# The softmax reciprocals of the forgetting attention, moved from VectorE to POOL as a power of minus one

## The chip, the cores and the metric

The kernel runs on one core of a Trainium2 chip. A core has five engines that run side by side, each with a queue of its own that is worked off in order: TensorE (PE in the profile, its weight loads PEld), VectorE (DVE), ScalarE (ACT), GpSimd (POOL) and SyncE (SP, which only issues transfers here). The metric is the device time of one execution in microseconds. Before the change the median of 3 runs was 1450.64 us (1450.14 to 1451.19).

## The reference

One encoder layer on x of 1024 tokens by 1024 channels, in float32: a mixer (forgetting attention beside gated linear attention), cross-attention to 256 memory tokens, and a squared-ReLU MLP, each behind an RMS norm and added to the residual. The change is in the forgetting attention (8 heads of 64 channels):

```python
for i in range(S // Q_BLOCK):                       # Q_BLOCK = 128
    start, end = i * Q_BLOCK, (i + 1) * Q_BLOCK
    s = jnp.einsum('bqhd,bkhd->bhqk', q[:, start:end], k[:, :end]) * scale
    bias = c[:, :, start:end, None] - c[:, :, None, :end]
    s = jnp.where(mask, s + bias, -jnp.inf)
    p = jax.nn.softmax(s, axis=-1)
    outs.append(jnp.einsum('bhqk,bkhd->bqhd', p, v[:, :end]))
```

A block of 128 queries sees only the keys up to its own end, so the eight blocks of a head are 128, 256, ... 1024 keys wide. The reciprocal in question is that of the softmax: one per query, 128 in a block, 64 blocks in all.

## The kernel before

All matrix products are float32 products made of three passes of split operands (`gemm`, L110 to L112). The stages follow each other: projections of the mixer (to about 315 us), forgetting attention (315 to 559 us), output projection, cross-attention (from about 600 us), and the MLP, which is more than half of the time.

The forgetting attention works by head, and in a head by blocks in the order 0, 4, 1, 5 (`fox_group` of group 0), then 2, 6, 3, 7. For each block `fox_scores` (L645 to L668) does this:

- TensorE writes the scores into PSUM (L656, L657, and the mask, L659). There is one PSUM tile for blocks of up to 512 keys (`s1`) and one for the wider ones (`s2`), so the next block of a kind waits until the exponential of the last one has read it.
- VectorE takes the negative row maximum (L661).
- ACT writes the exponential into `p` and sums it into `rs` (L664).
- VectorE takes the reciprocal of `rs`, 128x1 (L666).
- POOL multiplies `p` by it in place (L667).

Then `values` (L683) transposes `p` on TensorE (L696), ACT and VectorE split the transposes into a rounded part and a rest (`evac_split`, L117 and L118, three PSUM tiles `tr`), TensorE multiplies them with the values (L703, L704), and ACT and VectorE add the two halves (L706, L709).

Between these steps TensorE works on side work (`side_work`, L733): two parts of the output projection and the keys and values of the cross-attention. It is recorded in small pieces between the blocks, and its weights are loaded and split by ACT (L88) and VectorE (L93). At the end of the stage the first weights of the cross-attention are loaded and split (L80, L99, L100).

The order of instructions in a queue is not the order of the code. The program is built with `schedule_with_timeline_sim=True`: a scheduler plays the program with assumed durations and puts each engine's instructions in the order in which they come up there. An edit of a few lines can so move instructions of all engines. On the chip, each queue is then worked off in that fixed order.

POOL already has powers: `rstd` (L130) and its relatives (L345, L757, L861) raise a variance to -0.5, with a constant tile `mhalf` as the second operand.

Of the kernel before, what the change touches and what calls it, by code (L numbers as in the profile page):

```python
# [17 lines left out]
F32 = mybir.dt.float32  # L18
# [4 lines left out]
ALU = mybir.AluOpType  # L23
# [7 lines left out]
P = 128  # L31
# [20 lines left out]
class Layer:  # L52
# [194 lines left out]
    def consts(self, cp):  # L247
        nc = self.nc
        self.zerob = self.T(cp, [P, P], BF16, "zerob")
        nc.vector.memset(self.zerob, 0.0)  # L250
        self.cols = self.T(cp, [P, NCOLS], F32, "cols")
        self.ident = self.T(cp, [P, P], F32, "ident")
        make_identity(nc, self.ident)

        self.xv, self.xev, self.xr, self.xr2, self.hv, self.hev, self.hr, self.mv, self.mev, self.mr, self.yv = (
            self.T(cp, [P, NT], F32, n) for n in ("xv", "xev", "xr", "xr2", "hv", "hev", "hr", "mv", "mev", "mr", "yv"))
        self.mhalf = self.T(cp, [P, 8], F32, "mhalf")
        nc.vector.memset(self.mhalf, -0.5)
        self.identb = self.T(cp, [P, P], BF16, "identb")
        make_identity(nc, self.identb)  # L260
        self.maskb = self.T(cp, [P, P], BF16, "maskb")
        nc.gpsimd.memset(self.maskb, 0.0)
        nc.gpsimd.affine_select(out=self.maskb, in_=self.maskb, compare_op=ALU.is_ge, fill=NEG, base=0,
                                pattern=[[-1, P]], channel_multiplier=1)
        self.gfox = self.T(cp, [P, 64], F32, "gfox")
        self.gfk = self.T(cp, [P, 64], F32, "gfoxk")
        self.gx = self.T(cp, [P, 256], F32, "gx")
        self.ones = self.T(cp, [P, P], F32, "onesq")
        nc.gpsimd.memset(self.ones, 1.0)
# [375 lines left out]
    def fox_scores(self, h, t, A):  # L645

        nc, sps, p3 = self.nc, self.fox_s, self.fox3
        qa, qb, ka, kb, va = A
        ts, n = slice(t * P, (t + 1) * P), (t + 1) * P
        wide = n > 512  # L650
        ps = self.T(sps, [P, S if wide else 512], F32, "s2" if wide else "s1")
        for c0 in range(0, n, 512):
            w = max(min(512, n - c0), 256)
            c = slice(c0, c0 + w)
            last = c0 + 512 >= n
            nc.tensor.matmul(ps[:, c], qa[:, ts], ka[:, c], start=True, stop=False)  # L656
            nc.tensor.matmul(ps[:, c], qb[0:68, ts], kb[0:68, c], start=False, stop=not last)  # L657
            if last:
                nc.tensor.matmul(ps[:, ts], self.identb, self.maskb, start=False, stop=True)  # L659
        nm = self.T(self.smallp, [P, 1], F32, "nm")  # L660
        nc.vector.tensor_reduce(nm, ps[:, 0:n], AX.X, ALU.max, negate=True)  # L661
        p = self.T(p3, [P, S if wide else 512], F32, "p2" if wide else "p1")
        rs = self.T(self.smallp, [P, 1], F32, "rsum")
        nc.scalar.activation(p[:, 0:n], ps[:, 0:n], AF.Exp, bias=nm, accum_out=rs)  # L664
        rr = self.T(self.smallp, [P, 1], F32, "rrec")
        nc.vector.reciprocal(rr, rs)  # L666
        nc.gpsimd.tensor_scalar(p[:, 0:n], p[:, 0:n], rr, 1.0, ALU.mult, ALU.mult)  # L667
        return p  # L668

# [675 lines left out]
```

## Time and profile before

| | us |
|---|---|
| median of 3 runs | 1450.64 |
| the profiled execution | 1454.34 |
| its span, first to last instruction | 1452.6 |
| first of the 64 reciprocals starts at | 318.17 |
| last scaling of a block ends at | 553.16 |
| POOL busy in the whole span | 397.1 |
| VectorE busy in the whole span | 948.6 |

Times in the profile are counted from the first instruction. A row of the timeline has the start, the length, the engine, the line, the operation, its output and inputs with shapes, how often, and in brackets how long the engine was idle before and what ended that. Ends of matrix products are modelled: they overlap, and the distance of two starts tells their rate. "PEclk" is the clock that TensorE was granted, 1.00 being full speed.

### The profile page before, as it was taken

To read this page: it belongs to the slowest core of one execution; us is meant where nothing else is said; L and a number is where in the kernel's file an instruction comes from. 1 tells how busy PE (TensorE), PEld (TensorE's weight loads), DVE (VectorE), ACT (ScalarE), POOL (GpSimd) and SP (SyncE) were. 2 spreads that over 40 slices of the span, in tenths; PEclk is the share of its full clock that TensorE was granted. 3 is DMA by queue.
4 is the path that set the end of the run, shared out by engine and by line. 5 is a ranking of instruction groups with operands and counts; after the bars stand their busy time and mean duration, and the time that the engine had idled before them with its cause. 6 is when DMAs were issued, how large, how long until landed. Compare 5 with 4: busy or idle time off the path is not lost.

```text
span 1452.6 us, 19224 instructions
## 1 busy us (share of the span) xinstructions
PE 1427.7 (98%) x7068; PEld 1190.0 (82%) x7068; DVE 948.6 (65%) x1354; ACT 679.9 (47%) x1095; POOL 397.1 (27%) x404
## 2 busy tenths in 40 slices
PE   9999999998999999999999999999999999999998
PEld 7788788887888887888888878887888888888887
DVE  5366732428798776666644895636556968788796
ACT  4444341327678565455542364445546735335230
POOL 3235513312242223521212300000000542333454
PEclk9999999999999999999999999999999999999999
DMA  8435520268677642412474124444445835336353
GB/s 273 128 73 131 138 70 1 73 176 252 203 211 234 188 140 87 132 59 88 150 266 170 51 80 153 174 174 189 174 174 209 322 121 188 131 122 225 119 198 119
DMA packets 121166, 223.94 MB, mean 154 GB/s; under 512 B 8912, under 2 KB 54512, under 8 KB 118512
## 3 DMA queue, kind: packets, MB, share of 16 engines
q1 hardware_dynamic: 119776, 218.25, 46.5%
q10 hardware_dynamic: 1296, 4.46, 1.0%
q8 instruction: 56, 0.92, 0.3%
q14 instruction: 38, 0.31, 0.1%
HBM read 150.59 MB, written 72.09 MB: 153 GB/s over the span
## 4 chain that ended last, share of the span: by engine, by line
PE 71%; issue 16%; DMA 6%; DVE 3%; ACT 2%; POOL 1%; ACTq 0%; SPq 0%; DVEq 0%; POOLq 0%
PE mm L110 13%; PE mm L112 13%; PE mm L111 13%; PE my L111 5%; PE my L112 5%; PE my L110 5%; PE tr L111 2%; PE tr L112 2%; PE tr L110 2%; PE tr L696 2%; PE pv L703 1%; DMA xt<-in_x_dram 1%; DMA raw<-in_w_in_dram 1%; PE pv L704 1%; PE s L656 1%
## 5 line engine op out<-in xcount | busy, mean ns | idle before, releaser
L111 PE MATMUL my<-x,g 128*128 128x512 f32 x464 | 180.6, 389 | 1.3 <-DVE x L1076 1.3
L110 PE MATMUL my<-x,g 128*128 128x512 f32 x464 | 180.6, 390 | 0.4 <-ACT h L1281 0.4
L112 PE MATMUL my<-x,g 128*128 128x512 f32 x464 | 180.5, 389 | 0.0
L111 PE MATMUL mm<-wl,xh 128*128 128x512 f32 x320 | 126.5, 396 | 0.9 <-DVE wl L100 0.8
L110 PE MATMUL mm<-wh,xh 128*128 128x512 f32 x320 | 126.0, 397 | 1.0 <-DVE sq L307 1.0
L112 PE MATMUL mm<-wh,xl 128*128 128x512 f32 x320 | 125.9, 394 | 0.0
L1075 ACT ACTIVATE g<-s 128x1024 fp32r<-128x1024 f32 (+1 forms) x72 | 68.7, 962 | 105.0 <-PE my L112 39.1
L1076 DVE TENSOR_TENSOR g<-raw,g 128x512 fp32r<-128x512 f32 (+3 forms) x72 | 69.2, 964 | 67.6 <-ACT g L1075 67.4
L111 PEld LDWEIGHTS my<-x,g 128*128 128x128 f32 x464 | 87.1, 188 | 19.9 <-DVE x L1076 1.7
L1101 POOL TENSOR_TENSOR s<-raw 128x384 f32<-128x384 f32 (+1 forms) x20 | 25.8, 1291 | 282.7 <-DVE h L1196 213.8
L110 PEld LDWEIGHTS my<-x,g 128*128 128x128 f32 x464 | 87.1, 188 | 18.8 <-ACT h L1281 0.8
L1075 ACT ACTIVATE g<-raw 128x512 fp32r<-128x512 f32 (+3 forms) x72 | 55.5, 773 | 100.3 <-DMA raw<-in_mlp_w_dram 40.1
L112 PEld LDWEIGHTS my<-x,g 128*128 128x128 f32 x464 | 87.1, 188 | 17.9
L667 POOL TENSOR_SCALAR p<-p,rrec 128x128 f32<-128x128 f32 (+3 forms) x64 | 57.9, 907 | 159.2 <-DVE rrec L666 151.9
L1076 DVE TENSOR_TENSOR g<-s,g 128x1024 fp32r<-128x1024 f32 (+1 forms) x72 | 88.2, 1228 | 7.6 <-ACT g L1075 7.5
L1243 DVE TENSOR_TENSOR x<-x 128x1024 fp32r<-128x1024 f32 (+1 forms) x64 | 76.8, 1220 | 17.3 <-ACT x L1242 17.1
L110 PE MATMUL mm<-x,g 128*128 128x512 f32 x220 | 85.8, 390 | 0.0
L112 PE MATMUL mm<-x,g 128*128 128x512 f32 x220 | 85.7, 389 | 0.0
L111 PE MATMUL mm<-x,g 128*128 128x512 f32 x220 | 85.6, 389 | 0.0
L110 PE MATMUL tr<-x,g 128*128 128x512 f32 x212 | 82.5, 389 | 0.0
L111 PE MATMUL tr<-x,g 128*128 128x512 f32 x212 | 82.5, 389 | 0.0
L112 PE MATMUL tr<-x,g 128*128 128x512 f32 x212 | 82.5, 389 | 0.0
(318 smaller groups left out, 3739.2 us busy)
## 6 DMA issues: line engine op xcount, KB each, us to landing
ud<-h SPq DMA_DIRECT2D x32, 768.0 KB, 3.8
x<-ud SPq DMA_DIRECT2D x48, 512.0 KB, 5.3
raw<-in_mlp_w_dram SPq DMA_DIRECT2D x20, 1024.0 KB, 7.4
raw<-in_mlp_w_dram SPq DMA_DIRECT2D x16, 768.0 KB, 6.0
raw<-in_w_in_dram SPq DMA_DIRECT2D x23, 512.0 KB, 5.0
raw<-in_xattn_wkv_dram SPq DMA_DIRECT2D x16, 512.0 KB, 7.4
od<-o SPq DMA_DIRECT2D x32, 256.0 KB, 4.0
ud<-h SPq DMA_DIRECT2D x32, 256.0 KB, 2.8
```

The costliest lines, as they stand in the source:

```text
L110: mm(ps, lh[k], rh[k], start=start and k == 0, stop=False, **kw)
L111: mm(ps, lh[k], rl[k], start=False, stop=False, **kw)
L112: mm(ps, ll[k], rh[k], start=False, stop=stop and k == n - 1, **kw)
L656: nc.tensor.matmul(ps[:, c], qa[:, ts], ka[:, c], start=True, stop=False)
L667: nc.gpsimd.tensor_scalar(p[:, 0:n], p[:, 0:n], rr, 1.0, ALU.mult, ALU.mult)
L696: nc.tensor.transpose(o, pp[i][:, kb * P:(kb + 1) * P], self.ident)
L703: nc.tensor.matmul(pv, va[:, kb, :], th[:, js], start=kb == 0, stop=False)
L704: nc.tensor.matmul(pv, va[:, kb, :], tl[:, js], start=False, stop=kb == nb - 1)
L1075: self.nc.scalar.activation(hi, src, AF.Copy)
L1076: self.nc.vector.tensor_tensor(lo, src, f(hi), ALU.subtract)
L1101: eng.tensor_tensor(s[:, 0], raw[:, 3], raw[:, 2], ALU.add)
L1243: nc.vector.tensor_tensor(lo, f(lo), f(hi), ALU.subtract)
```

## The change

The reciprocal becomes a power with exponent -1 on POOL, with a constant tile `mone` of 128x1, filled once at the start. The scaling, on POOL before and after, now follows an instruction of its own engine.

```diff
         self.mhalf = self.T(cp, [P, 8], F32, "mhalf")
         nc.vector.memset(self.mhalf, -0.5)
+        self.mone = self.T(cp, [P, 1], F32, "mone")
+        nc.vector.memset(self.mone, -1.0)
...
         rr = self.T(self.smallp, [P, 1], F32, "rrec")
-        nc.vector.reciprocal(rr, rs)
+        nc.gpsimd.tensor_tensor(rr, rs, self.mone, ALU.pow)
         nc.gpsimd.tensor_scalar(p[:, 0:n], p[:, 0:n], rr, 1.0, ALU.mult, ALU.mult)
```

Lines behind the first edit count two higher in the changed kernel. VectorE has 64 instructions less and one more, POOL 64 more. The counts of TensorE, ACT and SP stay, but the scheduler orders them anew, from the first blocks of the stage to its end.

The first place is POOL's queue at the first blocks of head 0 (`p` with widths 128, 640, 256, 768 and 384). Before:

```order
L667 TENSOR_SCALAR p_444_2440<-p_444_2440,rrec_2443 128x128
L667 TENSOR_SCALAR p_449_2454<-p_449_2454,rrec_2457 128x640
L667 TENSOR_SCALAR p_454_2466<-p_454_2466,rrec_2469 128x256
L667 TENSOR_SCALAR p_459_2480<-p_459_2480,rrec_2483 128x768
L667 TENSOR_SCALAR p_547_2954<-p_547_2954,rrec_2957 128x384
```

and with the change:

```order
L668 TENSOR_TENSOR rrec_2445<-rsum_2443,mone_93 128x1
L669 TENSOR_SCALAR p_445_2442<-p_445_2442,rrec_2445 128x128
L668 TENSOR_TENSOR rrec_2459<-rsum_2457,mone_93 128x1
L669 TENSOR_SCALAR p_450_2456<-p_450_2456,rrec_2459 128x640
L668 TENSOR_TENSOR rrec_2471<-rsum_2469,mone_93 128x1
L669 TENSOR_SCALAR p_455_2468<-p_455_2468,rrec_2471 128x256
L668 TENSOR_TENSOR rrec_2485<-rsum_2483,mone_93 128x1
L669 TENSOR_SCALAR p_460_2482<-p_460_2482,rrec_2485 128x768
```

Each scaling has a power ahead of it; nothing else moved between them.

The second place is TensorE's queue near the end of the stage: the scores of the last block of head 6, which is 1024 keys wide (`s_1267` before, `s_1268` with the change), and the side work beside them (`mm_5458` and `mm_5460`, the last piece of the output projection, 18 products). Before:

```order
L659 MATMUL s_1262_5402<-maskb_98,identb_93 128x128
L656 MATMUL s_1267_5414<-ka_4905,qa_4903 128x512
L657 MATMUL s_1267_5414<-kb_4906,qb_4904 128x512
L656 MATMUL s_1267_5414<-ka_4905,qa_4903 128x512
L657 MATMUL s_1267_5414<-kb_4906,qb_4904 128x512
L659 LDWEIGHTS identb_93
L659 MATMUL s_1267_5414<-maskb_98,identb_93 128x128
L110 MATMUL mm_5458<-sh_5158,wh_4695 128x512
L111 MATMUL mm_5458<-sl_5159,wh_4695 128x512
L112 MATMUL mm_5458<-sh_5158,wl_4696 128x512
```

and with the change:

```order
L110 MATMUL mm_5460<-sh_5180,wh_4721 128x512
L111 MATMUL mm_5460<-sl_5181,wh_4721 128x512
L112 MATMUL mm_5460<-sh_5180,wl_4722 128x512
L698 MATMUL tr_5444<-ident_75,p_1255_5384 128x128
L658 MATMUL s_1268_5416<-ka_4907,qa_4905 128x512
L659 MATMUL s_1268_5416<-kb_4908,qb_4906 128x512
L658 MATMUL s_1268_5416<-ka_4907,qa_4905 128x512
L659 MATMUL s_1268_5416<-kb_4908,qb_4906 128x512
L661 LDWEIGHTS identb_95
L661 MATMUL s_1268_5416<-maskb_100,identb_95 128x128
L705 MATMUL pv_5312<-pth_5318,va_4904 128x256
L706 MATMUL pv_5312<-ptl_5319,va_4904 128x256
```

Before, the 18 side products begin behind these scores; with the change the last of them stands ahead of the scores, and products with values follow.

The third place is ACT's queue for the same block (`p_1269` before, `p_1270` with the change). Before:

```order
L88 ACTIVATE wh_5836<-raw_5834 128x512
L832 ACTIVATE sh_5848<-mixf_2768 128x512
L88 ACTIVATE wh_5840<-raw_5834 128x512
L832 ACTIVATE sh_5852<-mixf_2768 128x512
L664 ACTIVATE p_1269_5422,rsum_5423<-s_1267_5414,nm_5420 128x1024
L706 ACTIVATE ol_5350<-pv_5310 64x256
L99 ACTIVATE wh_6182<-raw_6180,cols_74 128x512
L99 ACTIVATE wh_6186<-raw_6180,cols_74 128x512
```

and with the change:

```order
L88 ACTIVATE wh_5842<-raw_5836 128x512
L834 ACTIVATE sh_5854<-mixf_2770 128x512
L99 ACTIVATE wh_6184<-raw_6182,cols_74 128x512
L99 ACTIVATE wh_6188<-raw_6182,cols_74 128x512
L708 ACTIVATE ol_5352<-pv_5312 64x256
L666 ACTIVATE p_1270_5424,rsum_5425<-s_1268_5416,nm_5422 128x1024
L117 ACTIVATE pth_5436<-tr_5431 128x512
L117 ACTIVATE pth_5449<-tr_5444 128x512
```

The two splits of the first weights of the cross-attention (L99), which wait for a load, and one addition (L706, now L708) moved from behind the exponential to ahead of it.

## The prediction

> **What bounds the kernel now.** I read the head of the profile's page first, then busy time by stage, then who waits for whom.
>
> ```profile
> span 1452.6 us, 19224 instructions
> PE 1427.7 (98%) x7068; PEld 1190.0 (82%) x7068; DVE 948.6 (65%) x1354; ACT 679.9 (47%) x1095; POOL 397.1 (27%) x404
> ```
>
> TensorE is busy for 98% of the span. Only what makes it wait, or lowers its clock, counts. The changed lines run between 318 and 553 us, so I cut that part into stages (length, busy time of PE, PEld, DVE, ACT and POOL, granted clock, DMA):
>
> ```profile
> 310.00:340.00 30.00, 26.34 (x120) 20.50 (x119) 15.89 (x30) 15.84 (x33) 5.04 (x6) 0.92 0.90 255
> 340.00:370.00 30.00, 29.55 (x177) 25.17 (x177) 23.01 (x47) 17.49 (x39) 8.95 (x8) 0.96 0.79 240
> 370.00:400.00 30.00, 28.88 (x171) 24.15 (x169) 22.62 (x45) 22.70 (x49) 8.95 (x16) 1.00 0.64 186
> 490.00:520.00 30.00, 30.00 (x184) 25.46 (x183) 23.26 (x45) 17.90 (x40) 7.02 (x9) 1.00 0.67 189
> 520.00:560.00 40.00, 35.85 (x230) 30.63 (x230) 32.68 (x63) 29.06 (x61) 9.69 (x11) 0.96 0.23 78
> ```
>
> TensorE idles 3.66 us in the first row, 0.45 and 1.12 in the next two, none at 490 to 520, and 4.15 in the last. These rows hold 9.4 us of idle time, at the two ends. VectorE is busy 75 to 82% in the later rows, POOL at most 30%. The clock is below 1 in the same two ends. Finer slices of the last one show how:
>
> ```profile
> 532.00:536.00 4.00, 3.06 (x21) 2.29 (x19) 4.00 (x9) 3.17 (x9) 1.13 (x1) 1.00 0.57 205
> 536.00:540.00 4.00, 3.75 (x18) 3.31 (x17) 3.02 (x9) 2.65 (x7) 1.45 (x3) 0.60 0.46 134
> ```
>
> After a slice with 0.94 us of idle TensorE, the next slice ran at 0.60, which costs 0.40 × 4 = 1.6 us. The first end costs 0.08 × 30 + 0.04 × 30 = 3.6 us in the same way. So idle time and clock together are some 9.4 + 5.2 = 14.6 us. That is about all that a change of these lines can win; what it can lose is bounded by no row. The waits between 310 and 560 us (us in total, times, longest):
>
> ```profile
> POOL p L667 <- DVE rrec L666: 151.9, 49, 13.8
> DVE rrec L666 <- ACT p L664: 11.8, 13, 1.7
> PE s L656 <- ACT p L664: 2.3, 4, 1.2
> PE tr L696 <- DVE ptl L118: 1.5, 1, 1.5
> PE pv L703 <- DVE mixf L709: 1.0, 1, 1.0
> PE tr L696 <- POOL p L667: 0.6, 2, 0.4
> ```
>
> POOL waits long for the reciprocals, but it has nothing else to do. TensorE waits only 0.6 us for the scaled tiles. At the 13 reciprocals in the second row VectorE stands still for the exponentials, 11.8 us in all; in the other 51 the sum was there first and the reciprocal queued behind VectorE's other work.
>
> **What goes.** 64 reciprocals leave VectorE.
>
> ```profile
> L666 DVE RECIPROCAL rrec<-rsum x64: 136/154/167, 318.2 to 551.7; 128x1 f32<-128x1 f32 x64
> L667 POOL TENSOR_SCALAR p<-p,rrec x64: 364/900/2262, 318.4 to 552.0; 128x128 f32<-128x128 f32 x8, 128x640 f32<-128x640 f32 x8, 128x256 f32<-128x256 f32 x8, 128x768 f32<-128x768 f32 x8
> ```
>
> 64 × 0.154 = 9.9 us of VectorE, and with it the 11.8 us of standing. In the middle, where TensorE has no idle time, this wins nothing: what is late next there is TensorE itself.
>
> **What comes.** 64 powers on POOL, each 128x1. The nearest rows are the same operation with exponent -0.5:
>
> ```profile
> L130 POOL TENSOR_TENSOR rs_r<-rs_v,mhalf 128x8 f32<-128x8 f32 x16 | 29.0, 1810 | 1.3
> L345 POOL TENSOR_TENSOR xr<-xv,mhalf 128x1 f32<-128x1 f32 x8 | 4.6, 574 | 0.5
> L137 POOL TENSOR_SCALAR xv<-ss 128x1 f32<-128x1 f32 x8 | 1.6, 204 | 22.1 <-ACT xsq L136 22.1
> ```
>
> I take 0.574 us (same operation, same shape), with bounds of 0.204 (a plain POOL operation of that shape) and 1.81 (the dearest power). That is 64 × 0.574 = 36.7 us of POOL, and 13 to 116 at the bounds. The memset of `mone` stands on VectorE at the very start, before its inputs have landed: nothing.
>
> **What one tile sees.** The scaling waits for the power on the same engine. A dependent pair on POOL:
>
> ```profile
> 601.74 0.27 POOL L129 TENSOR_SCALAR rs_v<-ss,hev 128x2 f32<-128x2 f32 x1 [1.99 <-DVE ss L146]
> 602.10 0.71 POOL L130 TENSOR_TENSOR rs_r<-rs_v,mhalf 128x2 f32<-128x2 f32 x1
> ```
>
> The second starts 0.09 us after the first ends. So from sum to scaling it will be about 0.05 + 0.57 + 0.09 = 0.7 us, if POOL is free. Before, it was anything between two kinds:
>
> ```profile
> 338.32 0.22 ACT L664 ACTIVATION_READ_ACCUMULATOR p<-s,nm 128x1 f32 x1
> 340.89 0.15 DVE L666 RECIPROCAL rrec<-rsum 128x1 f32<-128x1 f32 x1
> 341.14 2.26 POOL L667 TENSOR_SCALAR p<-p,rrec 128x512 f32<-128x512 f32 x1 [3.50 <-DVE rrec L666]
> 343.46 0.66 PE L696 MATMUL tr<-ident,p 128*128 128x128 f32 x4 [0.45 <-POOL p L667]
> 521.07 0.19 ACT L664 ACTIVATION_READ_ACCUMULATOR p<-s,nm 128x1 f32 x1
> 521.55 1.02 POOL L667 TENSOR_SCALAR p<-p,rrec 128x896 f32<-128x896 f32 x1 [1.79 <-DVE rrec L666]
> ```
>
> At 338.54 the sum stood ready and the scaling began 2.60 us later, because the reciprocal queued on VectorE. At 521.26 nobody was in the way, and it took 0.29 us. The queued kind gains up to 1.9 us, the free kind loses 0.4. Most tiles are of the queued kind, so on the mean the chain does not get longer; hardly any of this reaches TensorE.
>
> **First end.** The queued tile above made TensorE wait 0.45 us; that wait goes, and VectorE is two reciprocals earlier. The stall that lowers the clock comes ahead of it and stays. Term: **-0.5 us**, with bounds of 0 and -3.6 (the clock too).
>
> **Middle.** Cover is TensorE's own queue of side work. The order is redrawn there, and pairs of score blocks follow each other with no side work between. Term 0; bounds -1.6 (the idle time of the second and third stage) and +3 (two waits like the 1.5 us one, the longest for VectorE).
>
> **Last end.** Here the order matters, as the order listing shows: the 18 side products that followed the 1024-wide scores of head 6 now stand ahead of them. Before:
>
> ```profile
> 525.84 0.23 PE L659 MATMUL s<-maskb,identb 128*128 128x128 bf16 x1
> 525.88 0.48 PE L110 MATMUL mm<-sh,wh 128*128 128x512 f32 x1
> 528.50 0.39 PE L112 MATMUL mm<-sh,wl 128*128 128x512 f32 x1
> 527.24 1.22 DVE L661 TENSOR_REDUCE nm<-s 128x1 f32<-128x1024 f32 x1
> 529.14 3.20 SPq L80 DMA_DIRECT2D raw<-in_xattn_wq_dram  x2
> 530.03 1.10 ACT L664 ACTIVATE p<-s,nm 128x1024 f32<-128x1024 f32 x1
> 532.78 1.13 POOL L667 TENSOR_SCALAR p<-p,rrec 128x1024 f32<-128x1024 f32 x1 [2.58 <-PE tr L696]
> 532.81 1.34 ACT L99 ACTIVATE wh<-raw,cols 128x512 fp32r<-128x512 f32 x2 [0.81 <-DMA raw<-in_xattn_wq_dram]
> 533.96 0.55 PE L696 MATMUL tr<-ident,p 128*128 128x128 f32 x3 [0.18 <-POOL p L667]
> 557.33 0.28 PE L703 MATMUL pv<-pth,va 128*128 128x256 f32 x1
> 557.44 0.28 PE L704 MATMUL pv<-ptl,va 128*128 128x256 f32 x1
> ```
>
> From the end of the scores (526.0) to the transposes (533.96) are 8 us, and TensorE filled them with 18 side products of 2.62 / 11 = 0.238 us each (4.3 us) and with sums over values; it idled 0.18. After the change those 4.3 us are gone from behind the scores. The chain behind them is then at least maximum 1.2, exponential 1.3 with its read-out, power 0.7 with its step, scaling 1.1: 4.3 us. TensorE has 12 products with values there, at 0.12 each by the last two rows, and half a dozen transposes and the first scores of head 7 at about the same price: some 2.3 us. Besides, the exponential now stands behind two ACT operations that wait for a load (the row at 532.81 waited 0.81 for it), which adds up to 1 us. So 2 to 3 us are newly open. Against that, the same work was done earlier: the chain can start later in TensorE's queue and yet end only 1.8 to 2.8 us behind the old 533.96. From there both orders are the same chain of head 7, which had 0.32 to 1.49 us waits of its own for ACT and VectorE; eight reciprocals less shorten VectorE's part by 8 × 0.154 / 2 = 0.6 us (half of one overlaps its neighbour), and scores that were issued earlier give back about 0.5. Term: **+1.3 us**, with bounds of -3 (4.15 idle mostly gone) and +5 (4.3 uncovered and a slow clock of 1.6, less 0.6 and some).
>
> **A rule on the clock.** The row at 536 shows a slow stretch behind a slice with 77% busy. The Trainium skill, "TensorE: Matmul & The Clock Gate", Part 1, says that the clock falls to half only after a window of about 3.4 us without work. The trace doesn't agree on "idle": 3.06 busy of 4 us was enough here. By the Trainium skill the newly open wait of 2 to 3 us would cost no clock; by the row it costs one more stretch of 1.6 us.
>
> **The sum.** -0.5 + 0 + 1.3 = +0.8 us, against a profiled execution of 1454.34 us (span 1452.6, and 1.7 around it); the median of the runs is 3.7 us lower, 1450.64, and I set the difference on it: **1451.4 us**. About 0.2%, or 2.9 us, is what a measurement can tell here from no change.
>
> **Rivals.**
> - *The uncovered tile decides (slower).* TensorE idles 3 us or more between the last exponential of head 6 and its transposes, and a slow stretch follows: 1450.6 + 4.3 + 1.6 - 0.6 - 0.5 = 1455.3 us. It decides once that wait is over 2 us and the clock falls a second time. For it: the order. Against it: before, too, there was a slow stretch, and it may only move. Chance 0.28.
> - *The freed VectorE decides (faster).* VectorE is 4.00 busy of 4 us at 532 to 536 and the waits for it at 1.5 and 1.0 us shrink, one of the slow stretches does not come: 1450.6 - 2.5 - 1.6 - 0.5 = 1446.0 us. Against it: the 1.5 us wait stands behind a maximum and two subtractions, not behind reciprocals. Chance 0.18.
> - *The power is dearer than taken.* At 1.81 us a tile sees 1.2 us more, eight times in the last end, of which half is covered: 1451.4 + 5 = 1456 us. Chance 0.03.
> - *Every power lies on the path.* 64 × (0.574 - 0.154) = 26.9 us, so 1477.5 us; the 0.6 us that TensorE waits for scaled tiles speaks against it. Chance 0.01. The Trainium skill, "GPSIMD Engine Reference", § 4.1, puts elementwise work on VectorE and gives POOL as about twice as slow; the rows here say 3.7 times (574 to 154), and still hidden.
>
> **Numbers.** Forecast within 0.2%: 0.50. Slower: 0.28 + 0.03 + 0.01 = 0.32. Faster: 0.18. The range goes from 1447.0 (part of the freed VectorE) to 1456.0 (the uncovered tile with its clock), and leaves out about 0.1 on each side.
>
> **What would show it.** The powers at 0.5 to 0.65 us, scalings within 0.1 us behind them; VectorE some 10 us less busy; no wait of TensorE for POOL around 343; a wait of 1 to 3 us ahead of the transposes of head 6's last tile. Powers above 1 us, a stage from 346 to 520 with more than 3 us of idle TensorE, or a third slow stretch would make the forecast wrong.

## The result, and the profile after

The changed kernel took 1468.22 us (median of 4 runs, 1467.25 to 1470.21), the kernel before beside it 1450.91 us (4 runs, 1450.14 to 1454.31). The ratio is 1.0112, with a 95% interval of 1.0092 to 1.0132: some 16 us slower, where 1451.4 was forecast and 1456.0 was the end of the range.

The head of the page of the changed kernel:

```profile
span 1466.4 us, 19249 instructions
PE 1439.7 (98%) x7068; PEld 1188.9 (81%) x7068; DVE 945.2 (64%) x1291; ACT 681.9 (46%) x1095; POOL 428.3 (29%) x468
```

The span is 13.8 us longer, and TensorE's own busy time has grown by 12.0 us, with the same 7068 matrix products. That is not what a wait looks like: a wait would leave the busy time as it was. The reader's next question is where the busy time grew. The stages (length, busy time of PE, PEld, DVE, ACT and POOL, granted clock, DMA), of the changed kernel:

```profile
310.00:340.00 30.00, 25.79 (x118) 19.97 (x116) 14.98 (x23) 15.66 (x33) 10.06 (x13) 0.92 0.86 244
340.00:370.00 30.00, 28.76 (x174) 24.85 (x173) 23.35 (x41) 16.92 (x38) 8.94 (x14) 0.96 0.81 244
520.00:560.00 40.00, 35.17 (x245) 30.01 (x244) 32.90 (x54) 30.47 (x66) 18.56 (x26) 1.00 0.20 67
1100.00:1440.00 340.00, 340.00 (x1470) 275.50 (x1469) 267.53 (x296) 151.87 (x186) 124.49 (x89) 1.00 0.52 178
```

The first three answer to rows of before that the prediction shows; TensorE's busy time in them differs by under 1 us each. The fourth is a piece of the MLP, half a millisecond behind the changed lines. The same piece of the kernel before:

```profile
1100.00:1440.00 340.00, 339.64 (x1499) 280.92 (x1498) 266.33 (x299) 149.74 (x185) 131.43 (x93) 1.00 0.53 183
```

In 340 us TensorE started 1499 products before and 1470 after. The granted clock is 1.00 in both, TensorE is idle for at most 0.36 us, and nearly all of them are products of one shape (128x512). So one product takes 340 / 1499 = 226.8 ns before and 340 / 1470 = 231.3 ns after. Counted in starts of products, all of the trace behind the forgetting attention (from the 3000th product on) is 12.9 us longer; the part ahead of it is 1.1 us longer. In this pair of profiles the part with the forgetting attention grew by about what was forecast, and nearly all of the loss came from stages that the change doesn't touch.

### The profile page after: what moved, and what is told of

It is laid out like the page before. It is cut to its first block, busy times and chain, and to the rows that moved or that the text cites. A ratio compares the mean times of both kernels' runs of the same rounds, so it can differ in the third digit from the quotient of the medians.

```text
span 1466.4 us, 19249 instructions
## 1 busy us (share of the span) xinstructions
PE 1439.7 (98%) x7068; PEld 1188.9 (81%) x7068; DVE 945.2 (64%) x1291; ACT 681.9 (46%) x1095; POOL 428.3 (29%) x468
## 4 chain that ended last, share of the span: by engine, by line
PE 87%; DMA 5%; DVE 3%; ACT 2%; issue 1%; POOL 1%; ACTq 0%; DVEq 0%; POOLq 0%
PE mm L110 14%; PE mm L112 14%; PE mm L111 14%; PE my L111 7%; PE my L112 7%; PE my L110 7%; PE tr L110 3%; PE tr L112 3%; PE tr L111 3%; PE tr L698 2%; DMA xt<-in_x_dram 1%; DMA raw<-in_w_in_dram 1%; PE pv L705 1%; PE pv L706 1%; PE s L658 1%
## 5 line engine op out<-in xcount | busy, mean ns | idle before, releaser
L110 PE MATMUL mm<-wh,sh 128*128 128x512 f32 x192 | 77.0, 403 | 0.0
```

What stands on the lines that cost most here:

```text
L110: mm(ps, lh[k], rh[k], start=start and k == 0, stop=False, **kw)
```

## The theory, and what the trace could say of it

The order of instructions on TensorE is the same in both kernels behind the forgetting attention. What differs there is where the tiles lie. The tile `mone` has 4 bytes in each partition, takes 32, and stands in the first pool that is allocated; pools are stacked from the low end of the memory, some from the high end (`side="right"` in the code). So every tile stacked behind it from the low end lies 32 bytes higher, and those at the high end lie where they were. Addresses (bytes within a partition) in the two built programs:

| tile (pool) | used as | before | after | remainder of 256, before and after |
|---|---|---|---|---|
| `x7` (x0) | moving operand, MLP | 161760 | 161760 | 224, 224 |
| `x7` (x1, the first of 5) | moving operand, MLP | 9184 | 9216 | 224, 0 |
| `g1` (g74) | weights, MLP | 137184 | 137184 | 224, 224 |
| `g2` (g7a) | weights, MLP | 120800 | 120800 | 224, 224 |
| `g2` (g7b) | weights, MLP | 91104 | 91136 | 224, 0 |

A product reads one operand while it runs (the moving operand); the other, its weights, is loaded beside the running products (the rows of PEld). **Theory "placement"**: a product runs at 227 ns when its moving operand and the weights loaded beside it lie at the same remainder of some power of two, and slower when they don't (the expectations below call such a pair mixed). **Rival "order or power"**: the redrawn order, or the power on POOL, leaves something behind that slows the later stages. Of the trace of the changed kernel, the last 2400 products (the MLP) were grouped by the distance from the address of the next product's weights to that of the moving operand, less the whole multiples of 256 bytes ("modulo 256"; 224 is so also a distance of 32 the other way); the time is from a start to the next start, and gaps outside 215 to 245 ns are left out:

| kernel | distance modulo 256 | pairs | mean ns |
|---|---|---|---|
| before | 0 | 2363 | 226.7 |
| after | 0 | 1164 | 228.5 |
| after | 32 | 935 | 233.2 |
| after | 224 | 265 | 233.4 |

The built program has 2024 such pairs with a 512-wide moving operand at a distance other than 0 (40 before), most of them in the cross-attention and the MLP. 2024 × 6.5 ns = 13.2 us, close to the 12.9 us of the trace. A grouping is no proof, so the tile was tried apart from the power.

## The experiments

**e1: the tile without the power.**

```diff
         nc.vector.memset(self.mhalf, -0.5)
+        self.mone = self.T(cp, [P, 1], F32, "mone")
+        nc.vector.memset(self.mone, -1.0)
```

> The kernel before with only the tile mone and its memset added; the reciprocal stays on VectorE, and the order on TensorE, ACT, POOL and SP is that of before. Theory 'placement' (the new tile moves the tiles allocated behind it by 32 bytes, and a 512-wide matmul whose moving operand and whose successor's weights then start at different remainders of 64 bytes takes some 233 ns in place of 227): the program has 2009 such pairs, times 6.5 ns makes 13.1 us, so 1462 to 1467 us, with matmuls of the MLP at 231 ns on the mean after the fox stage. Theory 'order or power' (the new order, or the power on POOL, is what costs): same as before, 1450 to 1452 us.

Measured: 1463.65 us, ratio 1.0075 (1.0058 to 1.0092), so 11 us slower. TensorE, ACT, POOL and SP have the instructions of before in the order of before. The piece of the MLP, as above:

```profile
1100.00:1440.00 340.00, 340.00 (x1470) 275.59 (x1470) 268.22 (x295) 151.78 (x186) 124.78 (x91) 1.00 0.53 181
```

1470 products, as in the changed kernel; its pairs at distances of 32 and 224 took 233.2 and 233.4 ns, the same within a tenth or so, and from the 3000th product on its trace is 12.9 us longer than that of before, again as in the changed kernel. In the time of the runs, a constant that nobody reads costs some two thirds of the loss (11 of 16 us).

**e2: the power without the tile.** The exponent goes into a column of an old tile.

```diff
-        self.mone = self.T(cp, [P, 1], F32, "mone")
-        nc.vector.memset(self.mone, -1.0)
+        self.mone = self.yv[:, 0:1]
+        nc.vector.memset(self.yv, -1.0)
```

> The changed kernel with the exponent -1 kept in a constant tile that is there anyway (yv, not used before the MLP), so that no tile moves; powers and order are those of the changed kernel. 'Placement': 1450.5 to 1453 us, matmuls of the MLP back at 227 ns; what is left against before is the power and the order (forecast +0.8). 'Order or power': 1466 to 1469 us as in the changed kernel.

Measured: 1457.38 us, ratio 1.0024 (1.0014 to 1.0033): 3.5 us slower than before, with the order of the changed kernel. The piece of the MLP is back:

```profile
1100.00:1440.00 340.00, 339.06 (x1496) 280.49 (x1495) 266.43 (x299) 150.72 (x186) 131.09 (x92) 1.00 0.53 183
```

339.06 / 1496 = 226.6 ns. "Placement" is right for the large part. The 3.5 us are more than the forecast 0.8, and are taken up below (e7, e10 to e12).

**e3: a tile of 64 bytes.** `mone` gets 16 columns instead of 1 (the power reads the first), so that everything stacked behind it moves by 64 bytes.

```diff
-        self.mone = self.T(cp, [P, 1], F32, "mone")
+        self.mone = self.T(cp, [P, 16], F32, "mone")
```

> The changed kernel with the tile mone widened to 64 bytes per partition (one column is used), so that the tiles behind it move by 64 bytes in place of 32. 'Placement by the remainder of 64 bytes': no mixed pair, 1450.5 to 1453 us. 'Any move costs': 1464 to 1469 us. 'Order or power': 1466 to 1469 us.

Measured: 1467.99 us, ratio 1.0098 (1.0083 to 1.0113). The expectation for a grain of 64 (the power of two whose remainder counts) fell: pairs 64 bytes apart took 230.9 ns (935 pairs), 192 apart 233.1 (264). Either the grain is larger or any move costs.

**e4, e5, e6: the kernel before, with pools of the MLP moved.** Nothing else differs; the order on all engines is that of before. In e4 the pads are 8 and 8 columns (32 bytes each), in e5 32 and 64, in e6 128 and 64.

```diff
+        self.T(self.open(mx, "pa"), [P, 8], F32, "pa")
         x1 = self.open(mx, "x1", 5, **kw)
+        self.T(self.open(mx, "pb"), [P, 8], F32, "pb")
         gb = self.open(mx, "g7b", 2, **kw)
```

> The kernel before with only one pool moved by 32 bytes: x1, five operand tiles of the MLP (a pad of 32 bytes ahead of it and one behind it, so that the next pool moves by 64). Order and instructions are those of before. 'Placement': 1919 mixed 512-wide pairs, all in the MLP, times 6.5 ns is 12.5 us: 1461 to 1465 us; nothing before 840 us changes; matmuls from x1 at 233, from x0 at 227. 'Order or power': same as before, 1450 to 1452 us.

> The kernel before with two pools of the MLP moved: x1 by 128 bytes and g7b by 384 bytes (pads of 128 and 256 bytes), order and instructions as before. The pairs of moving operand and next weights then stand 128 bytes apart (mod 256) in 1346 cases, 256 apart in 862, and 0 in 474. 'Grain of 128': all at 227 ns, the time of before (1450 to 1455 us). 'Grain of 256': the 1346 pairs at 231 to 234, 1457 to 1462 us. 'Any distance other than a multiple of 1024 costs': 2208 pairs at 231 to 234, 1461 to 1467 us.

> The kernel before with x1 moved by 512 bytes and g7b by 768, order and instructions as before. The pairs then stand 256 bytes apart (mod 512) in 1152 cases and 0 or 512 apart in the rest. 'Grain of 128 or 256': the time of before. 'Grain of 512': 1152 pairs at 231 to 234, 1456 to 1461 us.

| kernel | distances modulo 256 other than 0 | such 512-wide pairs | their mean ns | ratio to before |
|---|---|---|---|---|
| e4 | 32, 192, 224 | 2248 | 232.7 to 233.2 | 1.0103 (1.0088 to 1.0118) |
| e5 | 128 | 1386 | 232.4 | 1.0056 (1.0035 to 1.0076) |
| e6 | none (distances of 0, 256, 512, 768) | 40 | – | 1.0009 (0.9994 to 1.0024) |

Each count includes some 40 pairs, most of them at a distance of 64, that the kernel before has too; the 40 of e6 are these.

e4 is slower still than expected, because its second pad put g7b at 64 bytes, which the grain of 64 called harmless. e5 rules out a grain of 128. In e6, pools moved by 512 and 768 bytes cost nothing that the interval tells from zero, and its pairs in the MLP took 226.7 ns: of the distances tried, only multiples of 256 are free. The loss goes with the count of pairs: 2248 × 6.5 ns = 14.6 us (measured 15.0), 1386 × 5.7 ns = 7.9 us (measured 8.1).

**e8 and e9: the change with its distances put right.** In e8 `mone` has 64 columns, 256 bytes (the power reads the first). In e9 it stays small, is put ahead of the other constants, and the high end gets a pad of 224 bytes (56 columns): every tile of the matrix products moves, and no distance changes modulo 256.

```diff
+            self.T(self.open(st, "pad", side="right"), [P, 56], F32, "pad")
             self.consts(self.open(st, "const"))
```

> The changed kernel with the tile mone widened to 256 bytes per partition (one column is used), so that the tiles behind it move by 256 bytes. 'Grain of 256' (pairs of moving operand and next weights at the same remainder of 256 bytes run at 227 ns, others at 231 to 234): the time of e2, 1455 to 1459 us, matmuls of the MLP at 227. 'Any move costs' or 'the tile mone as such costs': 1466 to 1469 us as in the changed kernel and in e3.

> The changed kernel with mone of 4 bytes (it takes 32), put ahead of the other constants, and a pad of 224 bytes at the other end of the memory, where some pools are allocated downward: both sides move, by +32 and -224 bytes, so that every distance is again what it was before modulo 256, while every address has another remainder. 'Distance decides': the time of e2, 1455 to 1459 us. 'The address as such decides': 1464 to 1469 us.

Measured: e8 1456.62 us, ratio 1.0025 (1.0009 to 1.0042); e9 1455.9 us, ratio 1.0014 (0.9994 to 1.0033). Pairs took 226.7 ns in both. The rows of the piece of the MLP, of e8 and then of e9:

```profile
1100.00:1440.00 340.00, 339.11 (x1497) 280.56 (x1496) 267.27 (x298) 151.26 (x186) 130.14 (x92) 1.00 0.54 183
```

```profile
1100.00:1440.00 340.00, 338.86 (x1495) 280.33 (x1495) 266.24 (x298) 151.06 (x186) 130.39 (x92) 1.00 0.53 183
```

For the pace of the products the distance decides, not the address, not the tile and not the power.

**e7, e10, e11: is the rest the length of the power, or the order?** In e7 a second power stands ahead of each. In e10 a product replaces the power, so that kernel leaves the reciprocal out and its numbers are not those of the attention. In e11 VectorE keeps the reciprocal, and a power whose result nobody uses stands on POOL ahead of each scaling. None of them moves a tile by other than a multiple of 256; in all three the scheduler drew a new order.

```diff
# e7
+        nc.gpsimd.tensor_tensor(self.yv[:, 1:2], rs, self.mone, ALU.pow)
         nc.gpsimd.tensor_tensor(rr, rs, self.mone, ALU.pow)
# e10
-        nc.gpsimd.tensor_tensor(rr, rs, self.mone, ALU.pow)
+        nc.gpsimd.tensor_tensor(rr, rs, self.mone, ALU.mult)
# e11
         nc.vector.reciprocal(rr, rs)
+        nc.gpsimd.tensor_tensor(self.yv[:, 1:2], rs, self.mone, ALU.pow)
```

> The kernel of e2 (no tile moves) with a second power ahead of each, whose result is not used: POOL carries 64 x 0.55 = 35 us more, and each scaling comes 0.64 us later; the scheduler draws the order anew. 'Power on the path' (the 3.5 us that e2 cost against before come from the power's duration): twice that and more, 1458 to 1464 us. 'Order' (they come from where the redrawn order put scores and ACT operations): within a few us of e2 with no such trend, 1450 to 1458 us.

> The kernel of e2 with a product in place of the power on POOL (the reciprocal is left out; the operation stands at the same place and takes some 0.2 to 0.3 us in place of 0.55); the scheduler draws the order anew. 'Length of the power': between before and e2, 1452 to 1456 us, at most a third of the loss of e2 left. 'Order': anywhere from 1450 to 1460, with TensorE's waits for the exponentials (ACT) and for the sums over values, not for POOL, making the difference.

> The kernel before with the reciprocal on VectorE as it was, and on POOL, ahead of each scaling, a power of the row sums whose result is not used (exponent in the old tile yv, so that no tile moves): VectorE keeps its work, POOL has 64 powers more; the scheduler draws the order anew. 'Length of the power on POOL': about e2, 1456 to 1459 us. 'Order': anywhere from 1450 to 1460 us, again by waits for ACT and for the sums over values.

Measured: e7 1461.88 us, ratio 1.0066 (1.0043 to 1.0088); e10 1464.23, 1.0072 (1.0054 to 1.0090); e11 1458.98, 1.0029 (1.0013 to 1.0045). e7 alone would speak for the length of the power. But e10 has the shortest operation of all and is the slowest; its time lies above the ranges of both expectations. e11 fits both, so it settles nothing by its time. The row of its product among the groups of the profile (busy, mean ns of one):

```profile
L668 POOL TENSOR_TENSOR rrec<-rsum,yv 128x1 f32<-128x1 f32 x64 | 16.2, 253 | 154.6 <-ACT p L666 153.6 <-PE s L661 0.9
```

That is less than half of a power (0.549 us in the changed kernel), and yet e10 is 0.72% slower than before where e2 is 0.24%. Its waits of TensorE between 310 and 565 us:

```profile
PE s L658 <- ACT p L666: 6.1, 7, 2.5
PE pv L705 <- DVE mixf L711: 2.3, 3, 1.2
PE tr L698 <- POOL p L669: 1.6, 3, 0.6
```

TensorE waits for the exponentials of ACT, 6.1 us against 2.3 before and 5.0 in e2, and for the scaled tiles only 1.6 (1.5 in e2). In e7, with twice the powers, it waits 4.8 us for ACT, 3.6 for `mixf`, and 1.8 for POOL; in e11 4.8 for ACT and 3.0 for POOL. TensorE's idle time from 310 to 565 us, all waits together, is 9.6 us before, 11.7 in e2, 13.9 in e11, 14.0 in e7 and 14.9 in e10. So the length of the power alone doesn't set what these kernels lose. That the order which each of them drew does is the likelier reading, but it is argued and not shown: an order could not be held fixed while the power was taken away, so how the 3.5 us split between the two is not measured.

**e12: a load of its own.** The trace shows one place where the order of e2 loses (see "The middle" below): a load that ACT waits for. Its tile shared a buffer with an earlier load; here it gets its own.

```diff
-            xt = self.T(mp, [P, D], F32, "memr")
+            xt = self.T(mp, [P, D], F32, "memq")
             nc.sync.dma_start(xt, self.mem[t * P:(t + 1) * P, :])
```

> The kernel of e2 with a tile of its own (4096 bytes, so remainders of 256 stay) for the second kind of loads of the cross-attention's memory (L754 in before), which so far had to wait until the tile of the first kind was free; the load can be issued earlier, and the scheduler draws the order anew. If the loss of e2 against before in the stretch from 343 to 380 us is the wait for this load ahead of the exponentials on ACT, that wait is gone or under 1 us and TensorE's wait for the sums over values at 370 with it: 1452 to 1456 us. If it is the order as such, the loss turns up elsewhere: 1455 to 1460 us.

Measured: 1456.86 us, ratio 1.0030 (1.0016 to 1.0044), as slow as e2. The stretches of e12 from 343 us on:

```profile
343.00:380.00 37.00, 37.00 (x234) 31.82 (x233) 28.28 (x48) 23.21 (x54) 17.27 (x27) 1.00 0.85 246
420.00:520.00 100.00, 98.41 (x579) 83.46 (x579) 71.28 (x115) 61.20 (x130) 40.71 (x51) 1.00 0.70 210
520.00:565.00 45.00, 39.13 (x243) 32.90 (x242) 33.44 (x54) 29.94 (x64) 17.38 (x24) 0.96 0.23 77
```

The idle time from 343 to 380 is gone altogether (1.47 us in e2, 3.24 in the changed kernel), and 1.59 and 5.87 us stand in the last two rows instead (e2: 0.22 and 4.90). The time lies in the range that was named for "the order as such", and the loss did turn up elsewhere, as was said for that case. That the load was the cause in this stretch fits, but e12 alone doesn't show it, since its order is new on all engines; the five profiles in "The middle" are the better evidence. No version beat the kernel before.

## Why the prediction was wrong, point by point

**The step that failed** is "The memset of `mone` stands on VectorE at the very start, before its inputs have landed: nothing." The memset does cost nothing. But the step priced the instruction and not the tile: 32 bytes at the head of the stack took 1.5% of the pace of TensorE in the rest of the kernel (12.9 us on 867.6 from the 3000th product on). e1 shows it by itself (+11 us; +12.9 in the trace behind the 3000th product), e2, e8 and e9 by taking it away. None of the rivals had it, since all of them looked for waits, and this loss has no wait in any row.

**The power** took 0.549 us in the middle (0.574 forecast), and the scaling comes 0.1 us behind it, as forecast. Of the changed kernel, the groups by tile (min, median and max ns) and one pair:

```profile
L668 POOL TENSOR_TENSOR rrec<-rsum,mone x64: 537/549/1077, 318.2 to 552.6; 128x1 f32<-128x1 f32 x64
L669 POOL TENSOR_SCALAR p<-p,rrec x64: 370/804/1922, 318.9 to 553.3; 128x128 f32<-128x128 f32 x8, 128x640 f32<-128x640 f32 x8, 128x256 f32<-128x256 f32 x8, 128x768 f32<-128x768 f32 x8
```

```profile
374.57 0.55 POOL L668 TENSOR_TENSOR rrec<-rsum,mone 128x1 f32<-128x1 f32 x1 [0.39 <-ACT p L666]
...
375.23 1.02 POOL L669 TENSOR_SCALAR p<-p,rrec 128x896 f32<-128x896 f32 x1
```

VectorE lost its 9.9 us of reciprocals; between 346 and 520 us it is busy 6.9 us less (135.5 to 128.6), over the whole span only 3.4, where some 10 were forecast. What filled the rest was not looked into.

**First end, middle, last end.** Five of the profiles have the order of before (before, e1, e4, e5, e6) and five that of the changed kernel (after, e2, e3, e8, and e9 but for one instruction of TensorE). TensorE's idle time in them, mean of five in us:

| stretch | order of before | order of the change | difference | forecast |
|---|---|---|---|---|
| 310 to 343 | 4.37 | 4.23 | -0.1 | -0.5 (first end) |
| 343 to 380 | 0.95 | 3.02 | +2.1 | 0 (middle) |
| 380 to 520 | 0.19 | 0.61 | +0.4 | 0 (middle) |
| 520 to 565 | 4.09 | 4.80 | +0.7 | +1.3 (last end) |

The sum is +3.1 us where +0.8 was forecast, and e2, e8 and e9 measure +3.5, +3.6 and +2.0 in time (the interval of e9 reaches to no change). The 3000th product starts at 578.9 us in the mean of the first five and at 581.8 in that of the others, though profiles of one order differ by 4 to 6 us there. So without the tile the change is slower by 0.1 to 0.25 per cent: the side with a chance of 0.32, though not by the mechanism of that rival. The term that was mis-sized is the middle, 0 with a bound of +3, measured +2.5. The wait of 0.45 us for POOL at 343 us went, as forecast for the first end, but the idle time there fell by only 0.1. (The sum of the first rival comes to 1455.4 us, not 1455.3; nothing hangs on it.)

**The middle.** "Cover is TensorE's own queue of side work" failed at two places. First, scores now follow scores of the same PSUM tile with no side work between, and wait for the exponential. Before, side work came right behind such scores:

```profile
344.92 0.23 PE L659 MATMUL s<-maskb,identb 128*128 128x128 bf16 x1
344.96 0.48 PE L110 MATMUL mm<-sh,wh 128*128 128x512 f32 x1
```

TensorE in the changed kernel:

```profile
345.31 0.23 PE L661 MATMUL s<-maskb,identb 128*128 128x128 bf16 x1
346.30 0.39 PE L658 MATMUL s<-ka,qa 128*128 128x256 f32 x1 [0.75 <-ACT p L666]
346.53 0.28 PE L659 MATMUL s<-kb,qb 68*128 68x256 f32 x1
346.65 0.23 PE L661 MATMUL s<-maskb,identb 128*128 128x128 bf16 x1
346.69 0.48 PE L110 MATMUL mm<-sh,wh 128*128 128x512 f32 x1
```

The side product at 346.69 could have filled the 0.75 us and stands behind. Second, at about 373 us TensorE waits for work that stands on ACT behind the square of the cross-attention's memory, and that square waits for a load. Both orders have this place. Before (VectorE's last reading of the tile that the load fills, the issue of the load, the square and TensorE):

```profile
361.47 1.90 DVE L121 SCALAR_TENSOR_TENSOR sl<-memr,cols,sh 128x256 fp32r<-128x256 f32 x4
363.40 0.43 SPq L754 DMA_DIRECT2D memr<-in_mem_dram  x1
365.49 0.33 SPq L805 DMA_DIRECT2D t2k<-in_xT_dram  x1
364.79 1.01 ACT L664 ACTIVATE p<-s,nm 128x896 f32<-128x896 f32 x1
370.20 1.06 ACT L136 ACTIVATE memr<-memr 128x1024 f32<-128x1024 f32 x1 [4.30 <-DMA memr<-in_mem_dram]
372.70 0.30 PE L696 MATMUL tr<-ident,p 128*128 128x128 f32 x1 [1.03 <-POOL mr L757]
```

and with the change:

```profile
362.69 1.66 DVE L121 SCALAR_TENSOR_TENSOR sl<-memr,cols,sh 128x256 fp32r<-128x256 f32 x4
365.44 0.33 SPq L807 DMA_DIRECT2D t2k<-in_xT_dram  x1
365.82 0.42 SPq L756 DMA_DIRECT2D memr<-in_mem_dram  x1
371.82 1.06 ACT L136 ACTIVATE memr<-memr 128x1024 f32<-128x1024 f32 x1 [6.35 <-DMA memr<-in_mem_dram]
372.99 0.38 ACT L708 ACTIVATE ol<-pv 64x256 f32<-64x256 f32 x1
373.40 1.01 ACT L666 ACTIVATE p<-s,nm 128x896 f32<-128x896 f32 x1
373.41 0.42 DVE L711 TENSOR_TENSOR mixf<-pv,ol 64x256 f32<-64x256 f32 x1 [3.56 <-ACT ol L708]
373.88 0.38 PE L705 MATMUL pv<-pth,va 128*128 128x256 f32 x1 [2.00 <-DVE mixf L711]
```

On ACT the square moved ahead of the 896-wide exponential, but TensorE's wait ends with the addition at 372.99, which stood behind the square before, too. What moved as well is the issue of the load. On SyncE a load of another tile (`t2k`) now stands ahead of it, and such loads wait there until a store of that tile has landed (7.4 us in three of them between 355 and 372 us of the changed kernel). In the five profiles with the order of before, the load is issued 0.02 to 0.03 us after VectorE has read the tile for the last time; in the five with the changed order, 0.7 to 2.0 us after. ACT waited 2.07 to 4.30 us for the load in the former, and 4.58, 6.35, 6.56, 6.88 and 7.05 us in the latter (e2, after, e8, e3, e9). TensorE's wait follows it: 0.3, 2.0, 2.2, 2.5 and 2.7 us, in each case some 4.3 less; with the order of before it is some 3.3 less than ACT's wait (1.03 for 4.30), or nothing. In e8, e3 and e9, the three with the longest waits, the granted clock from 343 to 380 us is 0.95, and 1.00 in the other seven; 0.05 × 37 = 1.9 us, a loss that the idle time above does not hold. e12, which issues the load at 343 us, has no idle time in the stretch.

**The last end.** A newly open wait of 1 to 3 us was forecast for the last block of head 6. It is there, 1.81 us, ahead of the next scores rather than the transposes; and the wait of 1.49 us for VectorE at 550 us is now one of 1.46 us for POOL. First the row of before, then the changed kernel:

```profile
550.78 0.84 PE L696 MATMUL tr<-ident,p 128*128 128x128 f32 x5 [1.49 <-DVE ptl L118]
```

```profile
536.96 0.51 PE L658 MATMUL s<-ka,qa 128*128 128x512 f32 x1 [1.81 <-ACT p L666]
538.29 0.39 PE L658 MATMUL s<-ka,qa 128*128 128x256 f32 x1 [0.27 <-ACT p L666]
...
551.91 0.77 PE L698 MATMUL tr<-ident,p 128*128 128x128 f32 x5 [1.46 <-POOL p L669]
```

The slow stretch at 536 did not come in this profile (the clock is 1.00 from 520 to 560), though the slice from 536 to 540 was busy for 2.77 of 4 us, less than the 3.06 that the prediction took to be enough for one. In e2, e3 and e9 the clock of 520 to 565 was 0.96, in e8 1.00, all with the same order. So the row that the prediction set against the Trainium skill's rule of an idle window ("TensorE: Matmul & The Clock Gate", Part 1) settles neither: a share of busy time in a slice does not tell when the clock falls.

## What to carry to other kernels

A tile is not free because its instruction is: a few bytes at the head of a stack of pools move everything behind them, so keep new constants in tiles that are there, or pad them to 256 bytes, and compare the count of products in a fixed stretch of an untouched stage before looking for waits. Where a scheduler draws the order, compare the orders of all queues before pricing the instructions of a small edit: the five orders drawn anew here were some 2 to 10 us slower than that of before, and not in the order of what the operation took. And look at the queue that issues the loads: a load that stands behind an issue that waits comes late, and so does all that stands behind the operation that waits for it.

## What the hardware showed unexpectedly

- The pace of the 128x512 products of float32 halves depends on the distance between the addresses of the moving operand and of the weights. In the last 2400 products it was 226.7 ns at multiples of 256 bytes, 233.2 at 32, 230.9 at 64, 232.4 at 128, 232.7 to 233.1 at 192, 232.9 to 233.4 at 224, at a granted clock of 1.00. The Trainium skill, "TensorE: Matmul & The Clock Gate", Part 2, says that loading the next tile's weights doesn't take read bandwidth from the running product; these runs don't agree with that as it stands: e4 and e6 have the same instructions in the same order and differ in the place of two pools alone, and e4 is slower by some 14 us (1.0103 and 1.0009 times before).
- Whether the weights in question are the product's own or the next one's is open: they mostly lie in one pool, and where only one of them was at another remainder than the moving operand (126 and 108 pairs in five kernels), both took 231 to 232 ns. What in the chip slows the product is open too. Pairs at a distance of 0 also slow a little, to 228.5, when others in the kernel do not fit; why was not tried.
